# Turning attention probabilities with square blocks and DMAs instead of TensorE, in a two-layer transformer trunk

## The chip, the cores and the metric

The kernel runs on one core of a Trainium2 chip. The metric is device time in microseconds (us) for one execution of the whole program. Engines are named as in the profile: PE (TensorE), DVE (VectorE), ACT (ScalarE), POOL (GpSimd) and SP (SyncE, which here only issues DMAs). Each engine takes its own instructions strictly in order, and waits on the others through semaphores.

## The reference

A decoder trunk of two layers in fp32, with one sequence of 256 tokens, model width 2048 and a feed-forward width of 8192. Layer 0 mixes tokens by "forgetting attention" with 16 heads of 128, layer 1 by a mixture of dilated windows with 8 heads, three score groups (dilations 1, 4, 16) and values of 256 per head. After each mixer comes an MLP with a squared ReLU. What matters here:

```python
def rms_norm(x, g):
    y = x * lax.rsqrt(jnp.mean(x * x, axis=-1, keepdims=True) + EPS)
    return y * g

def fox_attention(h, w_in, b_f, q_gain, k_gain, w_out):
    q, k, v, f = split(h @ w_in)                 # 16 heads of 128
    q, k = rms_norm(q, q_gain), rms_norm(k, k_gain)
    c = jnp.cumsum(jax.nn.log_sigmoid(f + b_f), axis=1)
    s = q @ k.T * dh ** -0.5 + c[query] - c[key]   # per head, causal
    p = jax.nn.softmax(s, axis=-1)
    return (p @ v) @ w_out

def dilated_attention(h, w_in, q_gain, k_gain, w_out):
    # per head: three groups of scores (window 128 steps of 1, 4, 16 tokens, ALiBi),
    # merged by their softmax denominators: one softmax over the union
    ...
    return o @ w_out

for i in range(2):
    x = x + mixer(rms_norm(x, mix_norm_g[i]))
    h = rms_norm(x, mlp_norm_g[i])
    x = x + jnp.square(jax.nn.relu(h @ w_up[i])) @ w_down[i]
```

## The kernel before, in words

**Products.** Nearly all the work is weights times activations. fp32 is reached with split operands: each weight tile and each activation is written as a high part (fp32r) and a low part, and a product is the sum of high x high, low x high and high x low, so three matmuls of 512 columns where one would be the exact product. `load` (its DMA is L287) brings 256 rows x 512 columns of weights, 512 KB, from DRAM into a tile `raw`; `split` makes `wh` from it (a cast on ACT, L308) and `wl` (the rest, the "cut", on DVE, L309). There are 801 such splits, five buffers for raw tiles and five for split ones, so the sixth load waits for the cut that frees its buffer. `product_steps` (L339 to L341) works through 16 steps of k with six matmuls each (two blocks of 128 tokens, three matmuls); one such step takes PE about 1.3 us, and is the clock by which everything else is placed.

**Placing the rest.** The order of instructions is made by a small planner, `Jobs`. Every chain of side work (a head, the turning of q and k, a norm) is a generator that runs beside the products: `yield 3` means to go on three steps later, and `yield ("fv", j)` to go on when the job with that key is done. The text of the engine queues is thus fixed when the program is built. `behind(...)` adds a scheduling order only: the instructions in it are placed behind the last one issued of a kind, such as the last cast or the last matmul of the product.

**Heads.** The forgetting layer runs in four groups j of four heads. For each group there is one product for q, one for k and one for v (96 matmuls each). The heads of group j run beside the q product of group j+1; those of group 3 run beside the first, paired steps of the output projection (`CUT` = 12 steps on two column blocks), which use the heads that are done. A `fox_head` waits for its q, k and masks, then for `4*hh + 2` steps (group 3: `3*hh + 2`), makes scores on PE, then maximum, exponential, sum and scaling on DVE and ACT, which leaves the probabilities `s`, 128 queries x 384 (first block: 128 keys of the first 128 tokens; then 256 keys of the second 128). Two steps later `p_transposed` (L591 to L601) lets PE transpose the three 128x128 blocks into PSUM (L594), and ACT and DVE split the first two into `p_hi` (L598) and `p_lo` (L599); ACT copies the third whole, `p_whole` (L600). After `yield ("fv", j)` and three steps, `pv` (L578 to L589) multiplies values by them. The dilated layer has four groups q4 of two heads, with three score groups each and two blocks of values; `dil_head` starts at `6*i + 2` steps, and its probabilities are called `p`.

**Transposition by square blocks.** The kernel already transposes its normalised activations (`transposed_by_dma`, L436 to L441) and the q and k heads (`qk_chain`, L539 to L544) without PE. DVE's stream transposition turns each 32x32 block in place; then four DMAs, one for each 32 partitions, write the turned blocks to a DRAM tile `blocks` so that their places are exchanged as well, and one DMA reads it back, 128 partitions in full rows. For q and k the four writes are issued by SP (L543), in the same queue as the weights' loads, and the read by POOL (L544). POOL also computes the power for the norm of q and k (`rq`, L525).

**PSUM.** Scores and the values' results take turns in two banks "sc", transposes in two banks "tp", products in four banks "acc".

Of the kernel before, what the change touches and what calls it, by code (L numbers as in the profile page):

```python
# [9 lines left out]
F32 = mybir.dt.float32  # L10
F32R = mybir.dt.float32r
I32 = mybir.dt.int32
# [5 lines left out]
P = 128  # L18
D = 2048
S = 256  # L20
# [3 lines left out]
KC = D // P  # L24
DFF = 4 * D
FH = 16
# [10 lines left out]
W_SUB = 2  # L37
RAW_SUB = 2
CUT = 12


class Jobs:
# [46 lines left out]
def trunk(ctx: ExitStack, tc, x, fox_w_in, fox_b_f, fox_q_gain, fox_k_gain, fox_w_out, dil_w_in,  # L89
# [34 lines left out]
    MLP_G, FOX_G, DIL_G = 2 * KC, 4 * KC, 4 * KC + 2  # L124

    def gain_rows(name, sources, queue=nc.sync):
        rows = work.tile([2 * KC, P], F32, tag="s", name=name, bufs=4)
        at = 0
        for src in sources:
            queue.dma_start(rows[at:at + src.shape[0], :], src)  # L130
            at += src.shape[0]
        return rows[0:at, :]
# [18 lines left out]

    def distances():

        di = work.tile([P, 3 * P], I32, tag="s", name="di", bufs=4)
        nc.gpsimd.iota(di[:, 0:P], pattern=[[-1, P]], base=0, channel_multiplier=1)
        nc.gpsimd.iota(di[:, P:3 * P], pattern=[[-1, 2 * P]], base=P, channel_multiplier=1)
        return di
# [29 lines left out]
    def dilation_tables():  # L187
        di = distances()
        yield 2
        df = work.tile([P, 3 * P], F32, tag="s", name="df", bufs=4)  # L190
        nc.vector.tensor_copy(df, di)
        for g, r in enumerate(DILATION):
            t = work.tile([P, 3 * P], F32, tag=f"t{g}", name=f"dist{g}")
            ok = work.tile([P, 3 * P], F32, tag="s", name=f"ok{g}", bufs=4)
            nc.vector.tensor_scalar(ok, df, 0.0, None, ALU.is_ge)
            nc.vector.tensor_scalar(t, df, float(SPAN * r), None, ALU.is_le)
            nc.vector.tensor_mul(ok, ok, t)
            yield 1
            if r > 1:
                ri = work.tile([P, 3 * P], I32, tag="s", name=f"ri{g}", bufs=4)  # L200
                nc.vector.tensor_scalar(ri, di, r - 1, None, ALU.bitwise_and)
                nc.vector.tensor_copy(t, ri)
                nc.vector.tensor_scalar(t, t, 0.0, None, ALU.is_equal)
                nc.vector.tensor_mul(ok, ok, t)
                yield 1
            nc.vector.tensor_mul(t, df, ok)
            nc.vector.tensor_scalar(ok, ok, -BIG, BIG, ALU.mult, ALU.add)
            nc.vector.tensor_add(t, t, ok)
            tables[g] = t
            jobs.done.add(("table", g))  # L210
            yield 1
# [363 lines left out]

    oT = {}

    def pv(pt_sb, vt, cols, o_hi, o_lo, name):  # L578
        for i, c in enumerate(cols):
            if i:  # L580
                yield 1
            po = ps_sc.tile([P, 512], F32, tag="sc", name=f"po_{name}_{i}")
            whole, v_hi, v_lo = vt
            p_hi, p_lo, p_whole = pt_sb
            for v, p, first in ((v_hi, p_hi, True), (v_hi, p_lo, False), (v_lo, p_hi, False)):
                nc.tensor.matmul(po[:, 0:S], v[:, c:c + P], in_turn(p, P), start=first, stop=False)
            nc.tensor.matmul(po[:, P:S], whole[:, c:c + P], p_whole, start=False, stop=True)
            nc.scalar.copy(o_hi[i], po[:, 0:S])
            nc.vector.tensor_sub(o_lo[i], po[:, 0:S], o_hi[i].bitcast(F32))  # L589

    def p_transposed(p, name):  # L591
        pt = ps_tp.tile([P, 3 * P], F32, tag="tp", name=f"ptp_{name}")
        for b in range(3):
            nc.tensor.transpose(pt[:, b * P:(b + 1) * P], p(b), ident)  # L594
        p_hi, p_lo = (work.tile([P, S], F32R, tag=f"pT{x}", name=f"pT{x}_{name}", bufs=2) for x in "hl")
        p_whole = work.tile([P, P], F32, tag="pTw", name=f"pTw_{name}", bufs=2)
        first = by_column(pt[:, 0:S], P)
        nc.scalar.copy(halves(p_hi, P), first)  # L598
        nc.vector.tensor_sub(halves(p_lo, P), first, halves(p_hi, P).bitcast(F32))  # L599
        nc.scalar.copy(p_whole, pt[:, S:3 * P])  # L600
        return p_hi, p_lo, p_whole  # L601

# [20 lines left out]
            nc.tensor.matmul(ps[:, P:3 * P], a[:, i, :], in_turn(b[:, i, :], P // 2), start=not onto and x == 0, stop=x == 2)  # L623


    def block(p_tile):
        at = (0, P, 2 * P)
        return lambda b: p_tile[:, at[b]:at[b] + P]


    c_q = const.tile([P, NT, FH], F32, name="c_q")

    negc = const.tile([P, 3 * P], F32R, name="negc")
# [7 lines left out]

    def gate_chain(tag, pf):
        yield (tag, "rstd")
        tri = work.tile([P, P], F32, tag="s", name="tri", bufs=4)
        nc.gpsimd.memset(tri, 1.0)
        nc.gpsimd.affine_select(out=tri, in_=tri, compare_op=ALU.is_ge, fill=0.0, base=0,
                                pattern=[[1, P]], channel_multiplier=-1)
        ones = work.tile([P, P], F32, tag="s", name="ones", bufs=4)
        nc.gpsimd.memset(ones, 1.0)
        f = work.tile([2 * FH, S], F32, tag="s", name="g_f", bufs=4)  # L650
        nc.vector.tensor_copy(f, pf)
        yield 3
        pft = ps_sc.tile([P, NT, 2 * FH], F32, tag="sc", name="pft")
# [35 lines left out]
        pct = ps_sc.tile([FH, S], F32, tag="sc", name="pct")  # L689
        for t in range(NT):  # L690
            nc.tensor.transpose(pct[:, t * P:(t + 1) * P], c_q[:, t, :], ident)
        ct = work.tile([FH, S], F32, tag="s", name="g_ct", bufs=4)
        nc.vector.tensor_scalar(ct, pct, -1.0, None, ALU.mult)
        zero = work.tile([P, 3 * P], F32, tag="s", name="g_zero", bufs=4)
        nc.vector.memset(zero, 0.0)
        nc.vector.tensor_copy(negc, zero)
        keys = by_column(ct, P // 2)
# [7 lines left out]
    def fox_head(j, hh, qT, kT, vt, sel):  # L705
        h = 4 * j + hh
        yield ("fq", j)
        yield ("fk", j)
        yield "gate"
        yield "mask"  # L710
        yield (3 if j == 3 else 4) * hh + 2
        ps = ps_sc.tile([P, 512], F32, tag="sc", name=f"sc_f{h}")
        with behind(issued["product"]):
            nc.tensor.matmul(ps[:, 0:3 * P], sel[:, hh, :], in_turn(negc, P // 2), start=True, stop=False)
        for t in range(NT):
            scores(ps, t, qT[hh // 2], kT[hh // 2], hh % 2, True)
        s = work.tile([P, 3 * P], F32, tag="s", name=f"s_f{h}", bufs=4)
# [12 lines left out]
        yield 1  # L730
        nc.vector.reciprocal(den, den)
        for t in range(NT):
            nc.vector.tensor_scalar_mul(s[:, spans[t]], s[:, spans[t]], den[:, t:t + 1])
        yield 2
        pt_sb = p_transposed(block(s), f"f{h}")
        yield ("fv", j)
        yield 3
        if ("f", h // 2) not in oT:
            oT["f", h // 2] = tuple(
                act.tile([P, 2, S], F32R, tag=f"aT{x}", name=f"oTf{x}_{h}", bufs=KC // 2) for x in "hl")  # L740
        hi, lo = oT["f", h // 2]
# [14 lines left out]
    def dil_head(q4, i, qTs, kTs, vt):  # L756
        h = 2 * q4 + i
        for g in range(3):
            yield ("dqk", q4, g)
        yield 6 * i + 2  # L760
        s = work.tile([P, 3, 3 * P], F32, tag="sd", name=f"sd{h}", bufs=1)
        for g in range(3):
            yield ("table", g)
# [18 lines left out]
        p = work.tile([P, 3 * P], F32, tag="s", name=f"p_d{h}", bufs=4)  # L782
        nc.vector.tensor_add(p, s[:, 0, :], s[:, 1, :])
        nc.vector.tensor_add(p, p, s[:, 2, :])
        for t in range(NT):
            nc.vector.tensor_scalar_mul(p[:, spans[t]], p[:, spans[t]], den[:, t:t + 1])
        yield 2
        pt_sb = p_transposed(block(p), f"d{h}")
        yield ("dv", q4)
        yield 2  # L790
        hi, lo = (act.tile([P, 2, S], F32R, tag=f"aT{x}", name=f"oTd{x}_{h}", bufs=KC // 2) for x in "hl")
        oT["d", h] = hi, lo
# [209 lines left out]
```

## Time and profile before

| what | value |
|---|---|
| median of three runs | 2161.17 us (2161.13 to 2162.83) |
| the profiled execution | 2161.91 us, span 2160.2 us |
| PE busy in the span | 2147.8 us, 11208 matmul instructions |
| DVE, ACT, POOL busy | 1397.9, 1105.9, 74.1 us |
| mean granted TensorE clock | 1.000 |
| DMA queue of SP | 446.27 MB, 66.1% of the 16 engines' time |

The profile is of one execution. In a group's row the first pair of numbers is the busy time in all and the mean of one instruction in ns, and the numbers behind the bar are the idle time of that engine just before, with what ended it. The busy times of pipelined matmuls overlap. In a timeline a row begins with the start and the duration in us. The rows of waits give, for a waiting engine and line and what released it, the sum in us, the number of times and the longest one.

### The profile page before, as it was taken

What the parts mean: (1) busy time and instruction counts of PE and PEld (TensorE: products, weight loads), DVE (VectorE), ACT (ScalarE), POOL (GpSimd) and SP (SyncE); (2) the same over time, 40 slices, a digit from 0 to 9 for tenths busy, and PEclk for the clock granted to TensorE, in tenths of its full rate; (3) what the DMA queues carried; (4) which work ended last, traced back from release to release, by engine and by line L of the source; (5) the groups of instructions that cost most, each with busy time, mean ns of one, the idle gap of its engine ahead of it and who ended that gap; (6) DMA issues with size and microseconds to landing.
All of it is one profiled execution on the core that took longest, in us unless ns stands there. A gap on an engine that the chain in (4) does not pass through costs nothing.

```text
span 2160.2 us, 30057 instructions
## 1 busy us (share of the span) xinstructions
PE 2147.8 (99%) x11208; PEld 1912.6 (89%) x11208; DVE 1397.9 (65%) x1862; ACT 1105.9 (51%) x1545; POOL 74.1 (3%) x92
## 2 busy tenths in 40 slices
PE   9999999999999999999999999999999999999999
PEld 7888888988998998998888888888988988988988
DVE  6777787765655565566668777676655655655664
ACT  6565655644544454455555565546544543544442
POOL 1111000000000000000011010100000000000000
PEclk9999999999999999999999999999999999999999
DMA  7676667766666666667776776758666666666664
GB/s 251 220 225 196 224 201 233 248 203 204 199 203 205 200 201 204 203 199 241 244 242 207 232 226 195 259 177 275 215 204 201 200 204 204 198 203 204 202 210 144
DMA packets 292354, 459.34 MB, mean 213 GB/s; under 512 B 21944, under 2 KB 104432, under 8 KB 292208
## 3 DMA queue, kind: packets, MB, share of 16 engines
q1 hardware_dynamic: 288416, 446.27, 66.1%
q0 software_dynamic: 3232, 10.50, 1.4%
q8 instruction: 87, 1.43, 0.3%
q10 hardware_dynamic: 560, 0.66, 0.1%
q14 instruction: 59, 0.48, 0.1%
HBM read 438.48 MB, written 18.87 MB: 212 GB/s over the span
## 4 chain that ended last, share of the span: by engine, by line
PE 92%; DVE 3%; DMA 2%; issue 1%; ACT 1%; POOL 0%; SPq 0%; DVEq 0%; ACTq 0%; POOLq 0%
PE acc L340 19%; PE acc L341 19%; PE acc L339 19%; PE up_n1a_acc L403 5%; PE up_n3a_acc L403 5%; PE up_n3a_sc L403 3%; PE up_n1a_tp L403 3%; PE up_n1a_sc L403 3%; PE up_n3a_tp L403 3%; PE up_n3a_acc L407 3%; PE up_n1a_acc L407 3%; DMA raw<-in_dil_w_in_dram 2%; DVE wl L309 1%; PE up_n3a_tp L407 1%; PE up_n1a_sc L407 1%; PE up_n1a_tp L407 1%
## 5 line engine op out<-in xcount | busy, mean ns | idle before, releaser
L309 DVE TENSOR_TENSOR wl<-raw,wh 128x1024 fp32r<-128x1024 f32 (+1 forms) x801 | 975.0, 1221 | 686.7 <-ACT wh L308 681.0
L308 ACT CAST wh<-raw 128x1024 fp32r<-128x1024 f32 (+1 forms) x801 | 837.7, 1048 | 931.7 <-PE acc L341 567.4
L339 PE MATMUL acc<-wh,hT_n 128*128 128x512 f32 x896 | 343.0, 384 | 0.5 <-ACT wh L308 0.5
L340 PE MATMUL acc<-wl,hT_n 128*128 128x512 f32 x896 | 339.9, 379 | 0.1
L341 PE MATMUL acc<-wh,hT_n 128*128 128x512 f32 x896 | 339.5, 379 | 0.0
L339 PE MATMUL acc<-wh,aTh_n1a 128*128 128x512 f32 x512 | 194.0, 379 | 0.0
L340 PE MATMUL acc<-wl,aTh_n1a 128*128 128x512 f32 x512 | 194.0, 379 | 0.0
L341 PE MATMUL acc<-wh,aTl_n1a 128*128 128x512 f32 x512 | 194.0, 379 | 0.0
L341 PEld LDWEIGHTS acc<-wh,hT_n 128*128 128x128 f32 x896 | 169.3, 189 | 24.1
L339 PEld LDWEIGHTS acc<-wh,hT_n 128*128 128x128 f32 x896 | 169.6, 189 | 23.4 <-ACT wh L308 0.9
L340 PEld LDWEIGHTS acc<-wl,hT_n 128*128 128x128 f32 x896 | 169.8, 190 | 22.6 <-DVE wl L309 0.4
L339 PE MATMUL acc<-wh,aTh_n3a 128*128 128x512 f32 x480 | 181.9, 379 | 0.0
L340 PE MATMUL acc<-wl,aTh_n3a 128*128 128x512 f32 x480 | 181.9, 379 | 0.0
L341 PE MATMUL acc<-wh,aTl_n3a 128*128 128x512 f32 x480 | 181.9, 379 | 0.0
L403 PE MATMUL up_n1a_acc<-hT_n,wh 128*128 128x512 f32 x512 | 181.6, 382 | 0.0
L403 PE MATMUL up_n3a_acc<-hT_n,wh 128*128 128x512 f32 x512 | 181.6, 382 | 0.0
L407 PE MATMUL up_n1a_acc<-hT_n,wl 128*128 128x256 f32 x512 | 139.6, 273 | 0.0
L407 PE MATMUL up_n3a_acc<-hT_n,wl 128*128 128x256 f32 x512 | 139.6, 273 | 0.0
L341 PEld LDWEIGHTS acc<-wh,aTl_n1a 128*128 128x128 f32 x512 | 96.8, 189 | 13.8
L340 PEld LDWEIGHTS acc<-wl,aTh_n1a 128*128 128x128 f32 x512 | 96.8, 189 | 13.7
L339 PEld LDWEIGHTS acc<-wh,aTh_n1a 128*128 128x128 f32 x512 | 96.8, 189 | 13.6
L403 PEld LDWEIGHTS up_n3a_acc<-hT_n,wh 128*128 128x128 f32 x512 | 96.8, 189 | 13.5
(725 smaller groups left out, 3202.3 us busy)
## 6 DMA issues: line engine op xcount, KB each, us to landing
raw<-in_mlp_w_up_dram SPq DMA_DIRECT2D x256, 512.0 KB, 4.1
raw<-in_mlp_w_down_dram SPq DMA_DIRECT2D x256, 512.0 KB, 4.2
raw<-in_dil_w_in_dram SPq DMA_DIRECT2D x192, 256.0 KB, 4.6
raw<-in_fox_w_in_dram SPq DMA_DIRECT2D x95, 512.0 KB, 4.1
raw<-in_fox_w_out_dram SPq DMA_DIRECT2D x32, 512.0 KB, 4.3
raw<-in_dil_w_in_dram SPq DMA_DIRECT2D x32, 512.0 KB, 4.4
raw<-in_dil_w_out_dram SPq DMA_DIRECT2D x32, 512.0 KB, 4.4
blocks_n<-turned_n SPq DMA_DIRECT2D x96, 64.0 KB, 2.4
```

The lines of the kernel that those rows point to most:

```text
L308: issued["cast"] = nc.scalar.copy(hi[:, part, :], raw[:, part, :])
L309: issued["cut"] = nc.vector.tensor_sub(lo[:, part, :], raw[:, part, :], hi[:, part, :].bitcast(F32))
L339: nc.tensor.matmul(acc[t], ah[:, tok], hi, start=first, stop=False)
L340: nc.tensor.matmul(acc[t], ah[:, tok], lo, start=False, stop=False)
L341: issued["product"] = nc.tensor.matmul(acc[t], al[:, tok], hi, start=False, stop=last)
L403: issued["product"] = nc.tensor.matmul(banks[b], hi[:, i, col], in_turn(tokens.rearrange("p x s -> p (x s)"), P // 2), start=first, stop=last)
L407: nc.tensor.matmul(banks[b][:, 0:S], lo[:, i, col], in_turn(tokens[:, 0, :], P // 2), start=False, stop=False)
```

## The change

For 21 of the 24 heads (forgetting heads 0 to 13 and dilated heads 0 to 6) PE's three transposes are replaced by the way that q and k already take: `p_turned` has one DVE stream transposition of 128x384, four writes by SP to a DRAM tile `pblocks` (48 KB each, in runs of 384 bytes) and one read by POOL's queue of 192 KB. After the values are ready and ten more steps, `p_split` makes `p_hi` (ACT, behind the last cast) and `p_lo` (DVE, behind the last cut) from the first two blocks; the third is used where it lies, so ACT's copy of it is gone. The heads f14, f15 and d7 keep PE's transposes.

`p_hi` and `p_lo` now lie in SBUF token block by token block. The matmuls in `pv` still stream both token blocks in turn (n outer, b inner, as `in_turn` did), so their result in PSUM has the two blocks interleaved; the matmul of `p_whole` writes every second column of PSUM, and the copies out of PSUM (`o_hi`, `o_lo`) read at a stride of two. In exchange the split of a head that PE transposes reads PSUM contiguously. `pv`'s matmuls are put behind the last matmul of the product.

The start of the heads: in group 3 of the forgetting layer 2, 4, 6 and 9 steps instead of 2, 5, 8 and 11; in the last dilated group 3*i + 2 instead of 6*i + 2; the others are as they were. The tiles of tag "s" get five buffers instead of four. In numbers: 63 PE instructions and 21 on ACT fewer, 21 on DVE, 84 DMAs of SP and 21 of POOL more.

```diff
+S_BUFS = 5
...
+    def by_token(po):
+        return po[:, 0:S].rearrange("p (n b) -> p b n", b=2)
+
     def pv(pt_sb, vt, cols, o_hi, o_lo, name):
...
-            for v, p, first in ((v_hi, p_hi, True), (v_hi, p_lo, False), (v_lo, p_hi, False)):
-                nc.tensor.matmul(po[:, 0:S], v[:, c:c + P], in_turn(p, P), start=first, stop=False)
-            nc.tensor.matmul(po[:, P:S], whole[:, c:c + P], p_whole, start=False, stop=True)
-            nc.scalar.copy(o_hi[i], po[:, 0:S])
-            nc.vector.tensor_sub(o_lo[i], po[:, 0:S], o_hi[i].bitcast(F32))
+            with behind(issued["product"]):
+                for v, p, first in ((v_hi, p_hi, True), (v_hi, p_lo, False), (v_lo, p_hi, False)):
+                    nc.tensor.matmul(po[:, 0:S], v[:, c:c + P], p.rearrange("p (b n) -> p n b", b=2), start=first, stop=False)
+                nc.tensor.matmul(by_token(po)[:, 1], whole[:, c:c + P], p_whole, start=False, stop=True)
+            hi, lo = (o.rearrange("p (b n) -> p b n", b=2) for o in (o_hi[i], o_lo[i]))
+            nc.scalar.copy(hi, by_token(po))
+            nc.vector.tensor_sub(lo, by_token(po), hi.bitcast(F32))
+
+    def p_turned(p, name):
+        turned = work.tile([P, 4, 3, 32], F32, tag="s", name=f"turned_{name}", bufs=S_BUFS)
+        nc.vector.transpose(turned.rearrange("p j b r -> p b j r"), p.rearrange("p (b j c) -> p b j c", b=3, c=32))
+        blocks = dram.tile([4, 32, 4, 3 * 32], F32, tag="pblocks", name=f"pblocks_{name}", bufs=4)
+        for i in range(4):
+            nc.sync.dma_start(blocks[:, :, i, :].rearrange("j c x -> c j x"),
+                              turned[32 * i:32 * i + 32].rearrange("p j b r -> p j (b r)"))
+        nc.gpsimd.dma_start(turned.rearrange("p i b r -> p (i b r)"), blocks.rearrange("j c i x -> (j c) (i x)"))
+        return turned
+
+    def p_split(turned, name):
+        p_hi, p_lo = (work.tile([P, S], F32R, tag=f"pT{x}", name=f"pT{x}_{name}", bufs=2) for x in "hl")
+        first = turned.rearrange("p i b r -> p b i r")[:, 0:2]
+        hi, lo = (x.rearrange("p (b i r) -> p b i r", b=2, i=4) for x in (p_hi, p_lo))
+        with behind(issued["cast"]):
+            nc.scalar.copy(hi, first)
+        with behind(issued["cut"]):
+            nc.vector.tensor_sub(lo, first, hi.bitcast(F32))
+        return p_hi, p_lo, turned[:, :, 2, :]
 
     def p_transposed(p, name):
...
-        first = by_column(pt[:, 0:S], P)
-        nc.scalar.copy(halves(p_hi, P), first)
-        nc.vector.tensor_sub(halves(p_lo, P), first, halves(p_hi, P).bitcast(F32))
+        nc.scalar.copy(p_hi, pt[:, 0:S])
+        nc.vector.tensor_sub(p_lo, pt[:, 0:S], p_hi.bitcast(F32))
         nc.scalar.copy(p_whole, pt[:, S:3 * P])
...
-        yield (3 if j == 3 else 4) * hh + 2
+        yield ((0, 2, 4, 7) if j == 3 else (0, 4, 8, 12))[hh] + 2
...
-        yield 2
-        pt_sb = p_transposed(block(s), f"f{h}")
-        yield ("fv", j)
-        yield 3
+        if j == 3 and hh > 1:
+            yield 2
+            pt_sb = p_transposed(s, f"f{h}")
+            yield 1
+        else:
+            turned = p_turned(s, f"f{h}")
+            yield ("fv", j)
+            yield 10
+            pt_sb = p_split(turned, f"f{h}")
+        yield 2
...
-        yield 6 * i + 2
+        yield (3 if q4 == 3 else 6) * i + 2
...
-        yield 2
-        pt_sb = p_transposed(block(p), f"d{h}")
-        yield ("dv", q4)
+        if (q4, i) == (3, 1):
+            yield 2
+            pt_sb = p_transposed(p, f"d{h}")
+        else:
+            turned = p_turned(p, f"d{h}")
+            yield ("dv", q4)
+            yield 10
+            pt_sb = p_split(turned, f"d{h}")
         yield 2
```

More of the change, by code (lines that the diff above doesn't have):

```diff
@@ L126, in gain_rows @@
     def gain_rows(name, sources, queue=nc.sync):
-        rows = work.tile([2 * KC, P], F32, tag="s", name=name, bufs=4)
+        rows = work.tile([2 * KC, P], F32, tag="s", name=name, bufs=S_BUFS)
         at = 0
@@ L152, in distances @@
     def distances():
-        di = work.tile([P, 3 * P], I32, tag="s", name="di", bufs=4)
+        di = work.tile([P, 3 * P], I32, tag="s", name="di", bufs=S_BUFS)
         nc.gpsimd.iota(di[:, 0:P], pattern=[[-1, P]], base=0, channel_multiplier=1)
@@ L189, in dilation_tables @@
         yield 2
-        df = work.tile([P, 3 * P], F32, tag="s", name="df", bufs=4)
+        df = work.tile([P, 3 * P], F32, tag="s", name="df", bufs=S_BUFS)
         nc.vector.tensor_copy(df, di)
@@ L193, in dilation_tables @@
             t = work.tile([P, 3 * P], F32, tag=f"t{g}", name=f"dist{g}")
-            ok = work.tile([P, 3 * P], F32, tag="s", name=f"ok{g}", bufs=4)
+            ok = work.tile([P, 3 * P], F32, tag="s", name=f"ok{g}", bufs=S_BUFS)
             nc.vector.tensor_scalar(ok, df, 0.0, None, ALU.is_ge)
@@ L199, in dilation_tables @@
             if r > 1:
-                ri = work.tile([P, 3 * P], I32, tag="s", name=f"ri{g}", bufs=4)
+                ri = work.tile([P, 3 * P], I32, tag="s", name=f"ri{g}", bufs=S_BUFS)
                 nc.vector.tensor_scalar(ri, di, r - 1, None, ALU.bitwise_and)
@@ L593, in p_transposed @@
         for b in range(3):
-            nc.tensor.transpose(pt[:, b * P:(b + 1) * P], p(b), ident)
+            nc.tensor.transpose(pt[:, b * P:(b + 1) * P], p[:, b * P:(b + 1) * P], ident)
         p_hi, p_lo = (work.tile([P, S], F32R, tag=f"pT{x}", name=f"pT{x}_{name}", bufs=2) for x in "hl")
-        p_whole = work.tile([P, P], F32, tag="pTw", name=f"pTw_{name}", bufs=2)
-        first = by_column(pt[:, 0:S], P)
-        nc.scalar.copy(halves(p_hi, P), first)
-        nc.vector.tensor_sub(halves(p_lo, P), first, halves(p_hi, P).bitcast(F32))
+        p_whole = work.tile([P, P], F32, tag="s", name=f"pTw_{name}", bufs=S_BUFS)
+        nc.scalar.copy(p_hi, pt[:, 0:S])
+        nc.vector.tensor_sub(p_lo, pt[:, 0:S], p_hi.bitcast(F32))
         nc.scalar.copy(p_whole, pt[:, S:3 * P])
@@ L623, in scores @@
             nc.tensor.matmul(ps[:, P:3 * P], a[:, i, :], in_turn(b[:, i, :], P // 2), start=not onto and x == 0, stop=x == 2)
-    def block(p_tile):
-        at = (0, P, 2 * P)
-        return lambda b: p_tile[:, at[b]:at[b] + P]
     c_q = const.tile([P, NT, FH], F32, name="c_q")
@@ L643, in gate_chain @@
         yield (tag, "rstd")
-        tri = work.tile([P, P], F32, tag="s", name="tri", bufs=4)
+        tri = work.tile([P, P], F32, tag="s", name="tri", bufs=S_BUFS)
         nc.gpsimd.memset(tri, 1.0)
@@ L647, in gate_chain @@
                                 pattern=[[1, P]], channel_multiplier=-1)
-        ones = work.tile([P, P], F32, tag="s", name="ones", bufs=4)
+        ones = work.tile([P, P], F32, tag="s", name="ones", bufs=S_BUFS)
         nc.gpsimd.memset(ones, 1.0)
-        f = work.tile([2 * FH, S], F32, tag="s", name="g_f", bufs=4)
+        f = work.tile([2 * FH, S], F32, tag="s", name="g_f", bufs=S_BUFS)
         nc.vector.tensor_copy(f, pf)
@@ L691, in gate_chain @@
             nc.tensor.transpose(pct[:, t * P:(t + 1) * P], c_q[:, t, :], ident)
-        ct = work.tile([FH, S], F32, tag="s", name="g_ct", bufs=4)
+        ct = work.tile([FH, S], F32, tag="s", name="g_ct", bufs=S_BUFS)
         nc.vector.tensor_scalar(ct, pct, -1.0, None, ALU.mult)
-        zero = work.tile([P, 3 * P], F32, tag="s", name="g_zero", bufs=4)
+        zero = work.tile([P, 3 * P], F32, tag="s", name="g_zero", bufs=S_BUFS)
         nc.vector.memset(zero, 0.0)
@@ L716, in fox_head @@
             scores(ps, t, qT[hh // 2], kT[hh // 2], hh % 2, True)
-        s = work.tile([P, 3 * P], F32, tag="s", name=f"s_f{h}", bufs=4)
+        s = work.tile([P, 3 * P], F32, tag="s", name=f"s_f{h}", bufs=S_BUFS)
         nm = small.tile([P, NT], F32, tag="nm", name=f"nm_f{h}")
@@ L781, in dil_head @@
         nc.vector.reciprocal(den, den)
-        p = work.tile([P, 3 * P], F32, tag="s", name=f"p_d{h}", bufs=4)
+        p = work.tile([P, 3 * P], F32, tag="s", name=f"p_d{h}", bufs=S_BUFS)
         nc.vector.tensor_add(p, s[:, 0, :], s[:, 1, :])
```

## The prediction

> **What bounds the kernel now.** I read the page's busy shares and its chain first, then the groups of instructions kept apart by shape, then TensorE's (PE's) timeline around one transposition, what PE waits for, and last SP's queue, because the change moves work there. From the page:
>
> ```profile
> PE 2147.8 (99%) x11208; PEld 1912.6 (89%) x11208; DVE 1397.9 (65%) x1862; ACT 1105.9 (51%) x1545; POOL 74.1 (3%) x92
> ...
> PE 92%; DVE 3%; DMA 2%; issue 1%; ACT 1%; POOL 0%; SPq 0%; DVEq 0%; ACTq 0%; POOLq 0%
> ```
>
> PE is the bound, at a granted clock of 1.000 throughout: 92% of the chain is its own work. So PE work that goes comes off the time almost whole, and other engines matter only where PE, which runs in order, comes to wait. The groups that the change touches, or that are nearest to what it adds:
>
> ```profile
> L594 PE MATMUL ptp_f<-ident,s_f 128*128 128x128 f32 x48 | 7.9, 273 | 0.0
> L594 PE MATMUL ptp_d<-ident,p_d 128*128 128x128 f32 x24 | 4.5, 286 | 1.1 <-DVE p_d L786 1.0
> ...
> L436 DVE STREAM_TRANSPOSE turned_n<-x 128x512 f32<-128x512 f32 x24 | 16.1, 691 | 0.0
> ...
> L598 ACT CAST pTh_f<-ptp_f 128x256 fp32r<-128x256 f32 x16 | 6.0, 372 | 10.8 <-PE ptp_f L594 10.8
> L600 ACT COPY pTw_f<-ptp_f 128x128 f32<-128x128 f32 x16 | 4.2, 264 | 15.5 <-DVE pTl_f L599 15.5
> ```
>
> The means overlap (matmuls are pipelined), so the price of a transposition is read from starts, in the timeline of one head's:
>
> ```profile
> 113.09 0.38 PE L341 MATMUL acc<-wh,hT_n 128*128 128x512 f32 x1
> 113.31 0.49 PE L594 MATMUL ptp_f<-ident,s_f 128*128 128x128 f32 x3
> 113.55 0.46 PE L339 MATMUL acc<-wh,hT_n 128*128 128x512 f32 x1
> 113.85 0.38 PE L340 MATMUL acc<-wl,hT_n 128*128 128x512 f32 x1
> ```
>
> A 512-column matmul starts 0.216 us after the one before it. From the transposes' start to the second matmul behind them are 0.54 us; less one step of 0.216, three transposes cost **0.33 us** of PE's queue, though nothing waited. What PE waited for, and the largest wait at a transposition:
>
> ```profile
> PE sc_d L620 <- DVE sd L769: 1.3, 2, 0.7
> PE sc_f L623 <- ACT fkT_0h L560: 1.1, 1, 1.1
> PE ptp_d L594 <- DVE p_d L786: 1.0, 1, 1.0
> PE acc L339 <- ACT wh L308: 0.5, 1, 0.5
> ...
> 1164.73 0.38 PE L341 MATMUL acc<-wh,hT_n 128*128 128x512 f32 x1
> 1166.12 0.70 PE L594 MATMUL ptp_d<-ident,p_d 128*128 128x128 f32 x3 [1.01 <-DVE p_d L786]
> ```
>
> So weights are hardly ever late now (0.5 us in all). SP's waits, its queue around the turning of group 1's queries, and the rows of DMA issues nearest to the new ones:
>
> ```profile
> SPq L287 <- DVE wl L309: 1177.7, 562, 4.8
> ...
> 115.74 0.37 SPq L287 DMA_DIRECT2D raw<-in_fox_w_in_dram  x1
> 117.75 1.79 SPq L543 DMA_DIRECT2D blocks_('fq', 1)_0_1282<-sq_('fq', 1)_0_1217  x4
> 120.08 1.76 SPq L543 DMA_DIRECT2D blocks_('fq', 1)_1_1289<-sq_('fq', 1)_1_1219  x4
> 121.93 2.32 SPq L287 DMA_DIRECT2D raw<-in_fox_w_in_dram  x2
> ...
> raw<-in_fox_w_in_dram SPq DMA_DIRECT2D x95, 512.0 KB, 4.1
> blocks_('fq', 1)_1_1289<-sq_('fq', 1)_1_1219 SPq DMA_DIRECT2D x4, 64.0 KB, 3.7
> qn_('fq', 1)_0_1276<-blocks_('fq', 1)_0_1282 POOLq DMA_DIRECT2D x1, 256.0 KB, 3.8
> ```
>
> SP issues one thing after another: raw weights (512 KB, each after the cut `wl` that frees its buffer) and the writes of turned blocks (four take about 1.8 us to issue). A raw load behind a write waits until that write's VectorE transposition is done.
>
> **The change, part by part.**
>
> *Transposes gone.* 21 heads x 0.33 = **-6.9 us** of PE's queue. With them go PE's pauses at three of the dilated heads, read from starts that are over their pitch: 1.39 - 0.22 = 1.17 us before 1166.12 and 0.15 behind it (d0), 0.28 + 0.15 (d2), 0.15 (d6): **-1.9 us**.
>
> *Work on VectorE and ScalarE.* Each of the 21 adds a 128x384 stream transposition (691 ns x 384/512, about 0.52 us estimated) and loses ScalarE's copy of the third block (0.26 us); the split into `p_hi` and `p_lo` (0.37 and 0.42 us) stays, from SBUF in runs of 32 elements, and reads of PSUM at stride 2 change places with contiguous ones. VectorE is busy 65%, ScalarE 51%; cuts end 5 to 12 us before PE uses them around the heads. That cover hides 0.5 us per head: 0. Without it, each head would cost up to 0.6 us, 12 us in all.
>
> *The way through DRAM.* Turned q and k go this way already: from the end of the stream transposition to the landing of the read were 6.7 to 10.5 us for the first of a pair, 9.3 to 13.4 for the second. A head needs 0.5 (transposition), 7 to 13, and up to 2 us for the two splits in turn behind casts and cuts: 8 to 16 us. Against that, from p ready (its time of before) to the place of its values' matmuls in the changed order lie 15.3 to 18.2 us of PE work (23.6 for f10). Tightest are d1, d3, d5 (15.3 to 15.8), whose reads can stand behind another wait in POOL's queue (the power L525). I take 0 to 0.3 us of PE waiting in all; the bounds are 0 and, if all took 16 us plus such a wait of 1.7, some 2 us for each tight head, 6 us. Behind a late `p` PE stops entirely, and behind a late split the next cast and cut.
>
> *Three heads that keep PE.* d7's start moves from 6i+2 to 3i+2 steps, so its transposes are reached about 1421.8 on before's clock, while its p is ready about 1423.5: **+1.7 us** (0 to 3.5, since the wait at its values' matmuls may add to it or go). f14's are reached at 306.5, its p is ready at 306 to 307: **+0.2** (0 to 0.5).
>
> *SP's queue.* 84 more writes of 48 KB, four per head, at 1.8 us of issue for four, 38 us in all: nothing by itself, SP waits 1177.7 us for cuts. But the order changes. Before, all raw loads that group 1's second half of the queries' product needs (the 36th to the 42nd) stood ahead of the writes of turned queries; after, the 40th to 42nd stand behind those and behind f3's. Then the 40th goes out when the writes do, at 122.3, lands at 126.4 (4.1), is cast (1.05) and cut (1.22) by 128.7, where PE wants it at 129.9: 1.2 us spare instead of 8.0. In group 2 likewise. In group 3 the four loads behind the writes are one step later, so the first is done at 265.9 while PE wants it at 263.3 to 264.6: **+1.3 to 2.6, I take 1.5**. The dilated groups have one load late with about 4 us spare: 0. The bounds for all groups are 0 (SP issues sooner than reckoned) and 6 (2 us worse than reckoned at each of the three).
>
> *Values' matmuls.* The same matmuls and columns; the third (`p_whole`, two passes) now writes PSUM at stride 2. No PE row writes so; those that read their moving operand at a stride step at 110 ns for 256 columns, as contiguous ones do. I take 0; at half rate 32 x 2 x 0.11 = 7.0 us is the upper end. No reason admits a gain.
>
> *DMA traffic.* 21 x 2 x 192 KB = 8.3 MB more on 459 MB, the DMA engines 66% busy: 0, hidden by raw loads that land some 7 us before their cast; at the other end 0.5 us on each landing, still hidden.
>
> Sum: -6.9 - 1.9 + 0.3 + 1.7 + 0.2 + 1.5 = -5.1 us. The profiled execution took 2161.9 (span 2160.2 and 1.7 around it), so 2156.8; the median shown stands 0.7 below it: **2156.1 us** (-0.23%). A measurement of this kernel tells 0.2% (4.3 us) from no change: 2156.9 is the border.
>
> **Rivals.**
>
> *Everything is hidden (0.13).* SP's order, d7 and f14 cost nothing: -8.8, 2152.4. For it: cuts are 5 us or more early everywhere; against it: d7's arithmetic.
>
> *Raw weights late at each fox group (0.22).* If each link of the estimate is 2 us worse, groups 1 and 2 stop PE 0.8 us each and group 3 some 3.5 to 4: -5.1 + 3.8 = 2159.9. For it: no load stood behind two heads' writes before; against: SP took a write 0.03 us after its transposition.
>
> *Short pieces (0.10).* The new writes are in runs of 384 bytes, those of before 512. If a landing took twice its 2.4 us, d1, d3 and d5 would lose about 1.5 us each: -5.1 + 4.5 = 2160.6. For it: nothing in the rows, as no write so short through this queue is priced there; against: 128 pieces per write, as before, and less data. The Trainium skill, "DMA: Bandwidth & Descriptors", Specifications, says that below 512 bytes a transfer is read, modified and written, and falls below the line rate; no run here shows it yet, and by it this would be the case.
>
> *Stride 2 at half rate (0.06).* +7.0: 2163.1.
>
> *Slower: p late at most heads (0.10).* PE must take the values' matmuls in their place. The room of 15.3 to 18.2 us is passed when the way through DRAM takes 16 us or more instead of 8 to 13, as by 4 us more at SP (a head's write behind a raw load that waits for its cut, 4.8 us at the longest). Beyond the border one more us costs about 20, one per head: at 17 us some 12 us in all, 2168. For it: SP's longest wait; against: its mean is 2.1.
>
> That PE's transposes go without effect is excluded by PE's 99%.
>
> **How the numbers follow.** My forecast, 2154 to 2158.5, has 0.39 (its waits all lie between 1.5 and 6 us); with the rivals that makes 1. Faster by over 0.2%: 0.13 + 0.39 less the part above the border (0.11) = 0.41, and some 0.06 of rivals that are only half as bad: 0.47. Slower by over 0.2% (over 2165.5): 0.10 and 0.04 from cases together. Same: 0.39. For 8 in 10 the range runs from 2151.5, just under all hidden, to 2165, which leaves out the slower case.
>
> **What would show it.** Steps right: PE's instructions 63 fewer, no `ptp` but f14, f15, d7; a wait of some 1.7 us at `ptp_d7`; PE waiting for `wl` or `wh` about 264 us and not near 130 and 190; waits at `po` under 0.5 us in all. Wrong if `po` waits for `pTl` at many heads, if the second pass of `p_whole` starts over 0.11 us after the first, or if the weights' waits come again in every group.

## The result and the profile after

The changed kernel takes 2175.48 us (median of six executions, 2171.82 to 2178.74), against 2161.59 for the kernel before (2161.07 to 2165.09): a ratio of 1.0064, with a 95% interval of 1.0053 to 1.0075. It is **14 us slower**; forecast were 5 us faster, and the range ended at 2165. The page of the changed kernel, busy shares and chain:

```profile
PE 2151.0 (99%) x11145; PEld 1911.4 (88%) x11145; DVE 1407.8 (65%) x1883; ACT 1101.1 (51%) x1524; POOL 85.1 (4%) x113
...
PE 86%; DVE 4%; issue 3%; DMA 3%; ACT 2%; POOL 1%; SPq 1%; POOLq 0%; DVEq 0%; ACTq 0%
```

PE has its 63 instructions fewer and is still called 99% busy, though the chain's share of it fell from 92% to 86%. That is the first thing to learn here: a PE that stands for 2 us here and there, some 13 us more than before by its rows of waits, does not show in a busy share of 2177 us. The chain's share is no measure either: a faster kernel below has 82%. What PE waited for shows it (waiting engine and line, releaser: us in total, times, longest):

```profile
PE po_d L593 <- DVE pTl_d L619: 6.9, 3, 2.5
PE sc_f L654 <- ACT fkT_0h L561: 4.0, 3, 1.8
PE po_f L593 <- DVE pTl_f L619: 2.7, 3, 1.0
...
PE sc_d L651 <- DVE sd L801: 1.8, 2, 1.5
PE po_f L593 <- ACT pTh_f L617: 0.5, 1, 0.5
PE po_d L593 <- ACT pTh_d L617: 0.5, 1, 0.5
PE acc L341 <- DVE wl L310: 0.5, 1, 0.5
```

Before, no such row named the values' matmuls (`po`); now they are 10.6 us, nearly all of it a wait for `p_lo` (`pTl`), three times in each layer. It is the sign that the prediction named for being wrong, `po` waiting for `pTl`, at six heads. By the starts of PE's matmuls these are f1, f5, f9 (1.0 to 1.2 us each), d0 (0.6 + 2.7), d2 (2.3) and d4 (2.4).

The second thing is in the windows by stage. Their columns are the stretch and its length, the busy times of PE, PEld, DVE, ACT and POOL with instructions, then the granted clock, the DMA share and GB/s:

```profile
1150.00:1200.00 50.00, 45.53 (x214) 39.07 (x213) 38.49 (x64) 26.64 (x44) 8.06 (x10) 0.93 0.71 214
1200.00:1300.00 100.00, 97.77 (x480) 85.75 (x479) 70.95 (x104) 55.29 (x81) 9.69 (x11) 1.00 0.71 224
```

The granted clock, 1.00 in every stage before, is 0.93 in the stage of d0, 0.97 from 300 to 350 us and 0.98 in the first 100. The timeline of PE at d0 shows what that is:

```profile
1189.33 0.38 PE L340 MATMUL acc<-wh,hT_n 128*128 128x512 f32 x1
1192.23 0.58 PE L593 MATMUL po_d<-pTl_d,dv0h 128*128 128x256 f32 x1 [2.52 <-DVE pTl_d L619]
1192.60 0.42 PE L593 MATMUL po_d<-pTh_d,dv0l 128*128 128x256 f32 x1
...
1193.67 0.63 PE L342 MATMUL acc<-wh,hT_n 128*128 128x512 f32 x1
1194.10 0.42 PE L593 MATMUL po_d<-pTh_d,dv0h 128*128 128x256 f32 x1
1194.31 0.42 PE L593 MATMUL po_d<-pTl_d,dv0h 128*128 128x256 f32 x1
```

Behind the wait a 512-column matmul takes 0.43 us from start to start instead of 0.216, and a 256-column one 0.21 instead of 0.11: half speed, until about 1198.3. The same follows the waits of 2.0 us at the scores of f0 (to 92.4) and of f12 (301 to 304). Summed over the starts, low clock cost some 6 us in this execution, and the mean clock of 0.997 says the same (0.003 x 2177 = 6.5). The six executions go with it: 2178.74, 2178.20 and 2177.95 at 0.997 to 0.998, 2171.82, 2172.74 and 2173.02 at 0.998 to 0.999.

Reckoned from PE's starts, each against the pitch of its shape, the 16.2 us that PE takes longer from its first to its last matmul are: -6.9 for the transposes, -1.9 for the pauses at them, +11.8 at the values' matmuls (the second value blocks of the dilated heads among them), +3.6 in group 3 (weights 0.6, f11's values 0.65, scores of f12 2.4), +6 by the clock, +1.6 at other scores, +0.5 at d7; small pauses make up the rest.

### The profile page after: what moved, and what is told of

Same layout as the page of the kernel before. It is cut to its first block, busy times and chain, and to the rows that moved or that the text cites. A ratio compares the mean times of both kernels' runs of the same rounds, so it can differ in the third digit from the quotient of the medians.

```text
span 2177.0 us, 30135 instructions
## 1 busy us (share of the span) xinstructions
PE 2151.0 (99%) x11145; PEld 1911.4 (88%) x11145; DVE 1407.8 (65%) x1883; ACT 1101.1 (51%) x1524; POOL 85.1 (4%) x113
## 4 chain that ended last, share of the span: by engine, by line
PE 86%; DVE 4%; issue 3%; DMA 3%; ACT 2%; POOL 1%; SPq 1%; POOLq 0%; DVEq 0%; ACTq 0%
PE acc L341 18%; PE acc L340 18%; PE acc L342 18%; PE up_n3a_acc L404 5%; PE up_n1a_acc L404 5%; PE up_n3a_sc L404 3%; PE up_n3a_tp L404 3%; PE up_n1a_sc L404 3%; PE up_n1a_tp L404 3%; PE up_n1a_acc L408 3%; PE up_n3a_acc L408 3%; DVE wl L310 2%; PE up_n1a_tp L408 1%; PE up_n1a_sc L408 1%; PE up_n3a_tp L408 1%
## 5 line engine op out<-in xcount | busy, mean ns | idle before, releaser
L404 PEld LDWEIGHTS up_n1a_acc<-hT_n,wh 128*128 128x128 f32 x512 | 96.8, 189 | 13.5
```

Source lines behind the costliest of these rows:

```text
L404: issued["product"] = nc.tensor.matmul(banks[b], hi[:, i, col], in_turn(tokens.rearrange("p x s -> p (x s)"), P // 2), start=first, stop=last)
```

## The experiments

Three causes can bring the waits at `po`. **A**: `p_lo` stands in VectorE's queue behind work that itself waits. **B**: the way through DRAM takes too long. **C**, for group 3: SP's 84 new writes put raw weights late. And **D**: the clock's fall is a cost of its own. The trace alone points to A. VectorE's timeline around d2's `p_lo`:

```profile
1260.58 0.17 DVE L524 TENSOR_SCALAR ss_('dqk', 2, 0)_11576<-ss_('dqk', 2, 0)_11576 128x8 f32<-128x8 f32 x1
1262.54 0.50 DVE L530 TENSOR_SCALAR rq_('dqk', 2, 0)_11580<-rq_('dqk', 2, 0)_11580,rstd_n 128x4 f32<-128x4 f32 x2 [1.79 <-POOL rq_('dqk', 2, 0)_11580 L526]
1262.80 0.69 DVE L532 TENSOR_TENSOR qn_('dqk', 2, 0)_0_11614<-acc,rq_('dqk', 2, 0)_11580 128x512 f32<-128x512 f32 x1
1263.41 1.22 DVE L310 TENSOR_TENSOR wl<-raw,wh 128x1024 fp32r<-128x1024 f32 x1
1264.54 0.42 DVE L619 TENSOR_TENSOR pTl_d<-turned_d,pTh_d 128x256 fp32r<-128x256 f32 x1
```

The read of d2's turned probabilities landed at 1255.5, and `p_hi` was done at 1261.4. `p_lo` then stood 3.2 us in VectorE's queue, behind the rescale of the next q and k (L530), which waits 1.79 us for POOL's power, behind a 0.69 us multiplication and a cut. PE had come for it at 1262.5 and waited until 1265.0.

**No way through DRAM.** `p_turned` does nothing but view the probabilities in another shape:

```diff
-        turned = work.tile([P, 4, 3, 32], F32, tag="s", name=f"turned_{name}", bufs=S_BUFS)
-        nc.vector.transpose(...)
-        ... four writes, one read ...
+        turned = p.rearrange("p (i b r) -> p i b r", i=4, b=3)
```

> The 21 heads are neither transposed by VectorE nor sent through DRAM: the probabilities are split where they lie, at the same step, so the output is not the reference's; all the rest is as in the changed kernel, and VectorE's queue still has p_lo of f1, f5, f9, d0, d2 and d4 behind the rescale that waits for GpSimd's power. Theory A (p_lo's place in VectorE's queue makes PE wait): PE's waits at the values' matmuls stay, 2 to 3 us at each of d0, d2, d4 and about 1 us at f1, f5, f9, 8 us or more in all. Theory B (the way through DRAM takes too long): they go, under 1 us in all, since nothing is on its way. Theory C (84 more writes in SP's queue make raw weights late in group 3): the wait for weights at 268 us, those at f10 and f11 and the 2 us at the scores of f12 go, because the raw loads stand ahead of the turned queries again. With A and C together the median is 2163 to 2170 us, with B and C 2152 to 2156.

2168.60 us (2168.08 to 2170.54), ratio 1.0038 [1.0023, 1.0053]. PE's waits in this kernel:

```profile
PE po_d L593 <- DVE pTl_d L613: 6.3, 3, 2.3
...
PE po_f L593 <- DVE pTl_f L613: 2.5, 3, 0.8
...
PE sc_f L648 <- ACT fkT_0h L561: 1.0, 1, 1.0
```

With nothing on its way through DRAM, 8.8 us of the waits at `po` stay, at the same six heads. So B falls for the changed kernel and A stands. The waits in group 3 are gone, as C says: the only row of waits at a forgetting head's scores that is left is f0's. VectorE's queue at d2 is the same picture:

```profile
1251.57 0.36 DVE L530 TENSOR_SCALAR rq_('dqk', 2, 0)_11436<-rq_('dqk', 2, 0)_11436,rstd_n 128x4 f32<-128x4 f32 x2 [1.85 <-POOL rq_('dqk', 2, 0)_11436 L526]
1251.84 0.69 DVE L532 TENSOR_TENSOR qn_('dqk', 2, 0)_0_11470<-acc,rq_('dqk', 2, 0)_11436 128x512 f32<-128x512 f32 x1
1252.44 1.22 DVE L310 TENSOR_TENSOR wl<-raw,wh 128x1024 fp32r<-128x1024 f32 x1
1253.58 0.42 DVE L613 TENSOR_TENSOR pTl_d<-p_d,pTh_d 128x256 fp32r<-128x256 f32 x1
```

**The split earlier.** Both kinds of heads. At 17 of the 21 heads, the six among them, the values' matmuls keep their place among the matmuls of the products; at f3, f7 and f11 they come 5 to 7 matmuls earlier, at f10 32 (6.9 us):

```diff
-            yield 10
+            yield 8
             pt_sb = p_split(turned, f"f{h}")
+            yield 2
         yield 2
```

> The split of p comes 8 steps after the head's values are ready instead of 10, and the values' matmuls 4 steps behind the split instead of 2, so PE's place for them is unchanged. That puts p_lo ahead of the rescale in VectorE's queue. Theory A: PE's waits at the values' matmuls fall from some 11 us to under 2 us, and the median by 8 to 13 us (to 2162 to 2167), with what the clock loses behind the long waits. Theory B: nothing gained or a loss, as p is wanted 2.6 us sooner. Theory C: group 3's waits (weights at 268 us, scores of f12 at 300 us) stay, some 3 to 5 us.

**2156.19 us** (2153.96 to 2162.29, ten executions), ratio 0.998 [0.997, 0.9989]: 19 us less than the changed kernel, more than expected, and faster than the kernel before. VectorE's queue at d2 (lines between are left out) has the two steps the other way round, and PE waits at `po` once, for 0.3 us:

```profile
1243.35 0.42 DVE L619 TENSOR_TENSOR pTl_d<-turned_d,pTh_d 128x256 fp32r<-128x256 f32 x1
1246.36 0.50 DVE L530 TENSOR_SCALAR rq_('dqk', 2, 0)_11584<-rq_('dqk', 2, 0)_11584,rstd_n 128x4 f32<-128x4 f32 x2 [1.78 <-POOL rq_('dqk', 2, 0)_11584 L526]
```

```profile
PE sc_d L651 <- DVE sd L802: 2.5, 3, 1.0
...
PE sc_f L654 <- ACT fkT_0h L561: 1.9, 3, 0.9
PE acc L340 <- ACT wh L309: 0.5, 1, 0.5
PE po_d L593 <- DVE pTl_d L619: 0.3, 1, 0.3
```

The clock is 1.000. Theory C's forecast fails here: PE waits for no weights in group 3 (the row for `wh` is a wait at 13 us), and at the scores of f12 for 1.0 us instead of 2.4, although SP issues the same writes. The way from the end of the stream transposition to the landing of the read is 6.3 to 10.4 us, the split comes at 7.6 to 13.4, and PE wants it at 11 to 15. At f2, f6, f10 and d1 ACT's part of the split now starts 0.08 us behind the landing: there the way has become the limit, and the split can't come earlier still.

**The six heads alone.** The same edit for f1, f5, f9, d0, d2 and d4 only (`yield 8 if h in (1, 5, 9) else 10`, and for the dilated layer `(0, 2, 4)`).

> The changed kernel with the early split (8 steps, then 4) for six heads alone: f1, f5, f9, d0, d2 and d4, whose p_lo stood behind the rescale in VectorE's queue. Theory A: their waits (some 10 us with what follows) go, and nearly the whole gain of the early split with them: 2158 to 2163, the rest being the late weights of group 3 and the scores of f12 (3.5 us and up to 1.5 by the clock). If the early split helps for another reason, that all heads have more time, at most a third of the gain comes: 2169 or more.

2159.40 us (2158.17 to 2161.84), ratio 0.9991 [0.9982, 1.0001]. Six heads carry 16 of the 19 us. The largest wait left at `po` is one of 1.4 us at d1, whose `p_lo` has two cuts (2.35 us) ahead of it and `p_hi` done since 1187.7; that is A's mechanism once more, with other work in front. No run keeps the place and takes POOL's wait away, so how much of a wait is the place and how much POOL's power is not separated.

**The values later.** `yield 4` instead of 2 between the split and the values' matmuls; the split stays at 10.

> Only the values' matmuls of the 21 heads come two steps later (4 behind the split instead of 2). Theories A and B both let PE's waits at them fall to under 1 us: the steps give 2.6 us, the longest wait was 2.7. Median 2162 to 2167. If p comes later still with more time (a queue that fills up), the waits come back. Group 3's waits stay by theory C.

2166.48 us (2164.81 to 2169.48), ratio 1.0028 [1.0016, 1.0039]. The time is in the expected range, 9 us better than the changed kernel, but the waits are not as expected: 3.6 us at `po` stay, where under 1 us was, 2.0 of them now for `p_hi`, and group 3 got worse. PE's waits:

```profile
PE sc_f L654 <- ACT fkT_0h L561: 4.7, 3, 2.7
...
PE po_f L593 <- ACT pTh_f L617: 2.0, 3, 1.0
...
PE po_d L593 <- DVE pTl_d L619: 1.6, 1, 1.6
...
PE acc L341 <- DVE wl L310: 0.9, 3, 0.4
```

The likely reading is that a PE that does not wait at f1, f5 and f9 comes earlier to the weights behind SP's writes: now these are late in each of the three groups (0.3 to 0.5 us), ACT waits 36.3 us for raw tiles of the forgetting layer (25.8 in the changed kernel, 5.7 before it), and `p_hi`, placed behind such a cast, is late with it. So C also works through A's kind of queue. It does not follow from the earlier PE alone: with the early split, where PE does not wait at these heads either, ACT waits 22.0 us and no weights are late.

**The writes on GpSimd's queue.** `nc.gpsimd.dma_start` for the four writes.

> The 84 writes of turned probabilities are issued by GpSimd instead of SP. SP's queue is then as before the change (eight raw loads of group 3 ahead of the turned queries), and in VectorE's queue p_lo of d0, d2 and d4 stands ahead of the rescale, that of f1, f5 and f9 behind it. Theory C: PE's waits in group 3 (weights at 268 us, scores of f12) go, 3.5 us and some 1.5 of low clock. Theory A: waits at d0, d2, d4 fall under 0.5 us each, those at f1, f5, f9 stay at about 1 us. Theory B: waits at d0, d2, d4 get longer, since four writes on GpSimd take over 2 us to issue. A and C: median 2158 to 2164; B: 2174 or more.

2161.10 us (2160.52 to 2162.94), ratio 1.0001 [0.9992, 1.001]. Group 3's waits go (no wait for `wl`, 0.9 us left at scores, f0's), and those at f1, f5 and f9 stay at 0.8 to 1.0, as A and C say. But this edit also moved `p_lo` of d0, d2 and d4 ahead of the rescale, so its 14 us are not C's alone; and at d0 and d3 about 1 us each is left, where under 0.5 was expected.

**Both mends.**

> Both mends at once: the split after 8 steps with the values' matmuls 4 behind it, and the 84 writes issued by GpSimd. If A and C are separate and add: no wait over 0.5 us at the values' matmuls (A) and none for weights or at the scores of f12 (C, 0.5 and 1.0 us with the split alone), so 1 to 2 us under the split alone: 2153.5 to 2155.5. If the writes on GpSimd make p late for the earlier split (theory B: some 2 us more on the way), waits come back at the values' matmuls of f2, f6 and f10, whose reads stand behind the power, and it is not faster than the split alone: 2156 to 2160.

2158.35 us (2156.86 to 2159.90), ratio 0.9987 [0.9978, 0.9996]. That is not faster than the split alone (2 us slower, with intervals that overlap), and here B is at work: with GpSimd issuing, the way takes 10.6 to 13.3 us for the forgetting heads f0 to f11 instead of 6.3 to 10.4, the split starts within 0.1 us of the landing at all of these, and PE waits again. By the starts of its matmuls that is at f3, f7 (2.5 us) and f11, where f2, f6 and f10 were expected:

```profile
PE po_f L593 <- ACT pTh_f L617: 3.0, 3, 2.5
...
PE sc_d L651 <- DVE sd L802: 2.5, 2, 2.0
```

**No way, and early.** The first edit and the early split together:

> As the run without the way through DRAM (the probabilities are split where they lie, so the output is not the reference's), but with the split after 8 steps and the values' matmuls 4 behind it. Theory A says that only the split's place made that run slow: PE's waits at the values' matmuls fall from 8.8 us to under 1 us and the median by 9 to 13 us, to 2155 to 2159; against the kernel with the way and the early split (2156.2) the rest is what the way itself still costs: 0 to 2 us, so 2154 to 2157. If something else in the shortened chain made it slow, the waits stay and the median is 2165 or more.

2153.71 us (2152.63 to 2156.45), ratio 0.9965 [0.9952, 0.9978], with no wait at `po`. This is a little under what was expected. Without the way, the gain at these places is 7.8 us, near the 8.8 of the sum's first two terms. With the way it is 4.9, so the way costs some 2.5 to 3 us; as the intervals of the two ratios overlap, this size is not sure.

**The parts alone.** One layer's heads as in the change, the other's as before it:

> Only the seven dilated heads go the new way; all 16 forgetting heads are transposed by PE, at the steps of before. By theory A the dilated part loses 12 us in waits and clock (d0 with the clock 6, d2 and d4 2.5 each, scores 1) and gains 7 x 0.33 + 1.9 = 4.2: some 2166 to 2170. By theory C alone (SP's queue) it would be 2157 to 2160, as the dilated groups have weights to spare.

> Only the 14 forgetting heads go the new way; all 8 dilated heads are transposed by PE, at the steps of before. By A, C and D this part loses 3.2 us at f1, f5 and f9, 3.6 in group 3, about 1 at the scores of f0 and f4 and up to 3 by the clock, and gains 14 x 0.33 = 4.6: 2164 to 2168. By A alone 2160 to 2162.

Dilated heads alone: 2171.90 us (2168.43 to 2173.51), ratio 1.0047 [1.0032, 1.0062], worse than expected; in the profiled execution the waits at d0, d2 and d4 were all followed by low clock. Forgetting heads alone: 2166.44 us (2162.47 to 2170.55), ratio 1.0022 [1.0012, 1.0031], in the range of A, C and D together; the profiled execution (2168.17) has no low clock, and a wait of 3.5 us at the scores of f12. So each layer loses by itself, 10.7 and 5.3 us.

**The clock.** Needless PE work in the waits, with everything else unchanged. The lines below fill those of d0, d2 and d4; the run with all heads changed has the same 16 transposes ahead of the scores of f0 and f12 as well:

```diff
+                    if name in ("d0", "d2", "d4") and i == 0 and p is p_lo:
+                        fill = ps_tp.tile([P, P], F32, tag="tp", name=f"fill_{name}")
+                        for _ in range(16):
+                            nc.tensor.transpose(fill, ident, ident)
```

> The changed kernel with 16 needless PE transposes (1.8 us of PE's queue) put into five of its longest waits: before the scores of f0 and f12, and before the matmul with p_lo of d0, d2 and d4. Theory D (behind a PE wait of about 2 us the granted clock falls, and the time it costs comes on top): the clock stays at 1.000 in all stages and the median falls by 2 to 5 us, to 2170.5 to 2173.5, although PE does more. Rival (the slow matmuls after a wait are the wait's own catching up, not the clock's): the median does not fall, 2175 or more, as the waits themselves end no sooner.

> The kernel in which only the dilated heads go the new way, with 16 needless PE transposes (1.8 us) ahead of the matmul with p_lo of d0, d2 and d4, inside PE's waits of 2.3 to 2.7 us. Theory D (the granted clock falls behind a wait of more than 2 us): the matmuls after these places are at full speed, clock 1.000 in the stages from 1150 to 1400 us where it was 0.97 and 0.98, and the median falls from 2171.9 by 3 to 5 us, to 2167 to 2169. Rival (no cost of the clock): 2171 to 2173, and with the transposes too long for the wait 2173 or more.

With all heads changed: 2175.30 us (2173.54 to 2180.56), clock 1.000 in the profile, so the clock was held, but the median did not fall: longer waits of 2.1 us appeared at f1 and at the scores of f4, where they had been 1.0 and 0.5. So this run does not settle the price. With the dilated heads alone: 2169.78 us (2168.51 to 2171.84), ratio 1.0038 [1.0024, 1.0052]. In the windows the kernel without the filling first, then the one with it:

```profile
1150.00:1200.00 50.00, 46.32 (x228) 39.76 (x227) 38.73 (x67) 26.57 (x44) 6.87 (x8) 0.97 0.70 222
1200.00:1300.00 100.00, 97.80 (x469) 85.77 (x468) 72.41 (x106) 57.54 (x87) 9.69 (x11) 0.98 0.71 224
```

```profile
1150.00:1200.00 50.00, 47.20 (x247) 40.98 (x246) 39.58 (x67) 28.24 (x47) 6.87 (x8) 1.00 0.72 219
1200.00:1300.00 100.00, 99.33 (x491) 87.47 (x490) 72.19 (x104) 57.88 (x87) 9.69 (x11) 1.00 0.74 234
```

The clock stays up behind the filled waits (the profiled execution of the filled kernel has one low stretch elsewhere, behind a wait of 2.7 us at f0); that part of D is shown. The median fell by 2.1 us where 3 to 5 were expected, and the two intervals overlap, so the price in time is shown only by the slow rows of the timeline, not by this comparison.

## Why the prediction was wrong, point by point

- **Transposes gone, -6.9 us: right.** PE's time less its pauses fell by 6.9 us, and the pauses at `ptp` of d0, d2 and d6 (-1.9) went.
- **The step that failed: the way through DRAM, costed at 0 to 0.3 us.** Its working set 15.3 to 18.2 us of room against 8 to 16 of need, counted from the time that p is ready, with "up to 2 us for the two splits in turn behind casts and cuts". The length was right (6.3 to 10.5 us measured, 7 to 13 assumed). But the split does not start when its data is there: its place in the queue is ten steps after the head, and what stands ahead there decides. For six heads that was a rescale waiting 1.6 to 1.8 us for POOL's power, for all of them casts and cuts, placed in PE's time. The splits began 11.5 to 17.9 us after the transposition (22.1 at f10), and only two steps, 2.6 us, lay between them and PE. I had looked up POOL's power as something that can delay a read in POOL's queue, and not who waits for it on VectorE. This cost 11.8 us at `po`, and a part of the low clock. The room was also over-sized at the dilated heads: with the early split, p is ready 12.4 to 14.1 us before PE's place at d0 to d5, not 15.3 or more. By the length of the way alone that would still have been enough.
- **SP's queue, +1.5 us (0 to 6): right in place and mechanism, too small.** The late loads of group 3 stopped PE 0.6 us at the weights, at 268.5 us. What I left out is what is late next: ACT waited 10.0 us for one raw tile, and `p_hi` of f10 and f11 stood behind the late casts (0.65 at f11); and the turning of group 3's k, for which POOL's reads went out at 287.4 and 291.0 instead of 281.1 and 282.7, so that f12's scores waited 2.4 us (2.0 and 0.4). In all this is 3.6 us in group 3. With the early split 1.0 of it is left, so SP's queue does not bring it alone: where the splits stand counts too.
- **The clock: missing altogether.** It is put at 1.000 in the prediction as if nothing could change it. Behind the waits at f0, f12 and d0 it was at half for 3.4, 3.4 and 6.8 us, some 6 us of time in the profiled execution.
- **d7 and f14, +1.7 and +0.2: too high.** PE waited 0.23 us at `ptp_d7` and 0.24 at its values, nothing at f14. The waits elsewhere are not the reason: with the early split, which has few, the wait at `ptp_d7` is 0.23 too. Which part of the estimate was too high stays open.
- **Values' matmuls writing PSUM at stride 2, 0: right.** The second pass starts 111 to 112 ns behind the first in 28 of the 32 matmuls before and in 30 after; the other two (214 ns) are d0's, in the low clock.
- **VectorE and ScalarE, 0: right for their length** (577 ns for the transposition, estimated 0.52; the split 401 and 417), and wrong for their order, which is the failure above.
- **Rivals.** Short pieces: refuted; the writes of 384-byte pieces landed after 1.7 and 1.8 us (medians of the two layers), the kernel's own of 512 after 1.7 to 3.5, and no penalty of the kind that the Trainium skill, "DMA: Bandwidth & Descriptors", Specifications, states for transfers under 512 bytes is to be seen in these rows, which differ in size too (48 and 64 KB). Raw weights late in all groups: came only when PE was made faster at `po`. "Slower: p late at most heads" has the sign, but its mechanism, the way being too long, is the one that the first experiment refutes, and at only six heads did PE wait for `p_lo` (f11's wait, in group 3, was for `p_hi`).
- The early split's 2156.2 us is within 0.1 of the number forecast. That is luck: it is another kernel than the one forecast, and its parts do not agree with the sum's either (no wait of 1.7 at d7, 2.5 at the dilated scores).

## What to carry to other kernels

When work moves between engines, ask for each new consumer not only when its data is ready, but what stands ahead of it in its own engine's queue at the place where the program puts it, and what that waits for in turn; here two steps earlier made 19 us of difference with the same instructions. Give the consumer's place slack on both sides, and check by leaving the transfer out: if the wait stays, the transfer was not its cause. Where an engine is busy 99%, look at the rows of waits and at the granted clock by stage instead.

## What the runs showed of the hardware

- The granted clock falls to half in pieces of fixed length. In the clock records of the 13 traces of this case it is 1.00 or 0.50; a low piece lasts 3.41 us or twice that, and in one trace the pieces begin whole multiples of 3.41 us apart (in the changed kernel at 88.98, 300.61 and 1191.49 us, 62 and 261 times 3.41). Cut into stretches on this grid, with the end of the program left out, the traces have ten stretches that a low piece follows, and in these PE stood still for 2.16 to 2.79 us by its starts. In none of the other stretches, from the start of the records some 12 us into the program, did it stand for more than 2.06 us. So it counts how much of a wait falls into one stretch: at d0 it was 2.4 us, while d2's wait of 2.33 us was divided, with 1.95 us in the larger part, and f12's of 3.5 us with the forgetting heads alone into 2.05 and 1.89, and neither was followed by low clock. The stretches of d0 (the next one is low) and of d2 (it is not):

```profile
1188.07:1191.49 3.42, 1.24 (x5) 0.79 (x5) 1.86 (x5) 1.28 (x3) 2.21 (x2) 1.00 0.71 183
1191.49:1194.90 3.41, 2.67 (x10) 2.49 (x11) 3.41 (x6) 0.37 (x1) 0.00 (x0) 0.50 0.18 55
...
1263.17:1266.58 3.41, 1.57 (x9) 1.46 (x10) 3.41 (x6) 0.85 (x2) 0.00 (x0) 1.00 0.31 93
1266.58:1269.99 3.41, 3.41 (x20) 3.05 (x19) 2.18 (x5) 1.43 (x2) 0.09 (x1) 1.00 0.49 117
```

  The same wait can thus cost nothing more, or 1.7 us (half of 3.41) and above, and executions of one kernel lie 6 us apart. This is read from the traces; no run shifted a wait against the grid. The Trainium skill, "TensorE: Matmul & The Clock Gate", Part 1, describes a gate that falls to half rate after an idle window of about 3.4 us that runs freely; the half rate and the window agree with that, but here a window in which PE stood for 2.2 us of its 3.4 was enough.
- With the four writes issued by GpSimd instead of SP, the way took 10.6 to 13.3 us instead of 6.3 to 10.4 at f0 to f11. Two things add up in the rows: a write landed 3.7 us after its issue (median of the forgetting heads) instead of 1.7, and the read of a head often stands in POOL's queue behind the first write of the next head, which waits for that head's transposition (f0's read went out at 100.1 us, right behind f1's first write at 99.5).
